# A two-block hybrid layer on one Trainium2 core: mixers that begin with keys and values, one scaling of the keys of both directions, and a planner that keeps two engines off one port

## Chip, core and metric

The kernel runs on one core of a Trainium2 chip. The metric is the device time of one execution in microseconds. Engines are named as in the profile: PE (TensorE matmul), PEld (its weight load), DVE (VectorE), ACT (ScalarE), POOL (GpSimd), SP (the queue that issues the DMAs).

## The reference

Two blocks run one after the other on `x` of 512 tokens by 1024, all in float32. The first mixes dilated attention, a gated linear attention and block attention, then a feed-forward net. The second has two layers (`DEPTH_2 = 2`); beside `x` it carries a context of 256 tokens, which leaves an output only in the first layer. A layer of the second block, cut to its core:

```python
ux = hx @ w_in[l]; uc = hc @ w_in[l]            # columns: fourier, q, k, v, two gates, i, hq, g
fx = fourier_mix(col(ux, OFF_FOURIER, FOURIER_W), w_four[l])
ax, ac = attention_group(ux, uc, ...)           # keys of context and x together
rx, rc = hgrn_group(ux, uc, ...)                # two directions, chunked scan
x = x + g_a * (jnp.concatenate([fx, ax, rx], axis=-1) @ w_out[l])
x = x + g_f * swiglu(rmsnorm_2(x) * (1 + sc_f) + sh_f, w_gate[l], w_up[l], w_down[l])

# one direction of the scan in hgrn_group (the second runs over flipped tokens):
cum = jnp.cumsum(lf, axis=2); last = cum[:, :, -1:, :]
s_new = jnp.exp(last[:, :, 0, :])[..., None] * s + einsum(kc * jnp.exp(last - cum), vc)
att = jnp.einsum('bhtd,bhsd,bhtsd->bhts', qc, kc, decay)   # decay = exp(cum_t - cum_s), causal
o = einsum(qc * jnp.exp(cum), s) + einsum(att, vc)
```

## The kernel before

**Order and planner.** The program is written as many small generators (tasks). `Sched.run` (L564) holds a clock for each engine, and at each step emits the operation that could start first by its own prices. An operation made by `alt(...)` may go to one of two engines, and the planner takes the one that would end sooner; `copy_any` is such a pair of DVE and ACT, and many `tensor_tensor` are pairs of DVE and POOL. What it emits is fixed: each engine executes its list in that order, and waits between engines are semaphores on data alone. So prices and rules of the planner change no arithmetic, but they set the order on each engine and which engine gets an operation. All instructions show line 543, the one line that emits them.

**The flag that the change sets.** An `Op` has a mark `port` (L242): true for a POOL operation with an input, and for a DVE operation with two or more SBUF inputs that are more than one column wide, or a DVE copy or `tensor_scalar` from SBUF to SBUF. `emit` notes in `s.port` when the last such operation of DVE and of POOL ends. With `LOCK` true, `run` (L595) lets a marked operation begin, in the plan, only after the last marked one of the other engine. With `LOCK` false it ignores them.

**The second block's mixers.** `layer` (L2543) spawns the tasks and feeds matrix products to PE through `mix_in` (L2321). That takes the column groups of `w_in` in a fixed order: four gates first, then `ORDER2` (L150): `i` (the scan's values), `kv`, `hq` (the scan's queries), `q0`, `fo`, `q1`, `g`. `prep` (L157) lays the weights out in memory in the same order. The context of layer 0 runs earlier, between pieces of the first block, in its own order `ORDER2C`. `kv_to` (L1919) normalises the keys per head on DVE, ACT and POOL; `stack_k` (L795) then transposes them on PE, splits them in two parts and copies halves across partitions by DMA. Weights come as 512 KB tiles (`raw`), which ACT and DVE split into two parts (`wu`).

**The scan.** `hgrn` (L2094) runs, for two pairs of heads (`hgp`), one task `seg` for each 256 tokens. A segment holds `K` (keys of both directions side by side, 256 columns each), `Q`, and decay products. It climbs seven levels, `lev` = 1, 2, 4, ... 64. At each level it copies the keys that are needed together (`bidir_gram`, L2058), forms 32 thin products on PE (`low_gram`, 16 for each of two heads; `cross_grams` from level 32 on), and scales keys and queries by decay products (`bidir_level`, L2042) for the next level. The segments with an output are 2 for the context in layer 0 and 4 for `x` in each layer; layer 1's context has 2 without an output. All are chains: a level's products need the level before. PE's list puts dense products of other tasks between the thin ones.

Of the kernel before, what the change touches and what calls it, by code (L numbers as in the profile page):

```python
# [13 lines left out]
ALU = mybir.AluOpType  # L14
# [3 lines left out]
P = 128  # L18
T = 512
TC = 256  # L20
# [89 lines left out]
def tilesA(w):  # L110
    k, n = w.shape
    return w.reshape(k // P, P, n // P, P).transpose(2, 1, 0, 3).reshape(n // P, P, (k // P) * P)
# [23 lines left out]
def pairs(units):  # L136
    return np.ascontiguousarray(np.concatenate(units, 0))
# [9 lines left out]

FF1 = (4,) * 8
FF2 = (4, 4, 4, 4, 6)
ORDER2 = ("i", "kv", "hq", "q0", "fo", "q1", "g")  # L150
ORDER2C = ("i", "kv", "hq", "g", "q0", "q1", "fo")
ORDER1 = ("q", "k", "v0", "p0", "v1", "v2", "p1", "p2", "p3", "v3", "p4", "p5", "r0", "r1")
QPERM = np.concatenate([np.concatenate([np.arange(64 * j, 64 * j + 64), np.arange(64 * (j + 4), 64 * (j + 4) + 64)])
# [3 lines left out]
def prep(i):  # L157
# [40 lines left out]
    for l in range(2):  # L198
# [6 lines left out]
        a[f"w2in{l}"] = pairs([tilesA(x)[t:t + 1] for t in range(2) for x in (ff, fb)]  # L205
                              + [parts[n] for n in ORDER2])
        wo = i["w_out_2"][l]
# [90 lines left out]
def _op(eng, fn, args, kw):  # L298
    aps = [x for x in args if is_ap(x)] + [x for k, x in kw.items() if is_ap(x) and k != "accum_out"]
    outs = keys(args[0])  # L300
    if "accum_out" in kw:
        outs += keys(kw["accum_out"])
    if fn == "tensor_tensor_reduce":
        outs += keys(args[-1])
    ins = all_keys(aps[1:])
    n = max(free_size(a) for a in aps)
    table = None
    if eng == "dve":
        per = 1.04
        if fn in ("tensor_copy", "tensor_scalar", "memset") and not any(in_psum(a) for a in aps):  # L310
            per = 0.52
        if fn == "reciprocal":
            per = 6.6
        cost, lat = 62 + n * per + 62 * any(is_ap(a) and free_size(a) == 1 and n > 1 for a in args[2:]), 130
    elif eng == "act":
        extra = sum(1 for k in ("bias", "scale") if is_ap(kw.get(k))) + (fn == "mul" and is_ap(args[2]))
        cost, lat = 90 + n / 1.2 + 90 * extra + (60 if "accum_out" in kw else 0), 160
        for a in args:
            if not is_ap(a) and a in TABLES:
                table = TABLES[a]  # L320
    elif eng == "pool":
        cost, lat = 115 + n * (2.15 if fn == "tensor_tensor" else 3.7), 150
        if fn == "memset":
            cost = 200 + n
    elif eng == "sp":
        b = 4 * free_size(args[0]) * args[0].shape[0]
        cost, lat = max(b / 360.0, 460), 2300
    else:
        raise ValueError(eng)
    op = Op(eng, [(fn, args, kw)], cost, lat, ins, outs, table)  # L330
    if eng == "dve":

        sb = sum(1 for a in aps[1:] if not in_psum(a) and free_size(a) > 1)
        op.port = sb > 1 or (fn in ("tensor_copy", "tensor_scalar") and sb > 0 and not in_psum(args[0]))
    return op


def V(fn, *a, **k):
    return _op("dve", fn, a, k)
# [6 lines left out]
def G(fn, *a, **k):  # L346
    return _op("pool", fn, a, k)
# [6 lines left out]
def alt(*ops):  # L354
    ops[0].alt = ops[1:]
    return ops[0]
# [44 lines left out]
def zigzag(v, off, dims):  # L401

    return bass.AP(tensor=v.tensor, offset=v.offset + off, ap=[list(v.ap[0])] + [list(d) for d in dims if d[1] > 1 or d is dims[-1]])
# [32 lines left out]
class Sched:  # L436
# [127 lines left out]
    def run(s):  # L564
        while s.tasks:
            best = None
            progress = False
            for t in list(s.tasks):
# [22 lines left out]
                if isinstance(p, Op):  # L591
                    first = None
                    for o in (p,) + tuple(p.alt or ()):
                        ready = s.ready_of(o)
                        if LOCK and o.port:  # L595
                            ready = max(ready, s.port["pool" if o.eng == "dve" else "dve"])
# [27 lines left out]
class Kernel:  # L624
# [1417 lines left out]
    def bidir_level(s, K, Q, src, so, nbl, tot, no, lev):  # L2042


        m = nbl // 2
        sv = src[:, so:so + 2 * nbl].rearrange("p (d b two) -> p d b two", d=2, two=2)
        for d in range(2):
            kv = K[:, d * TC:(d + 1) * TC].rearrange("p (b two l) -> p b two l", two=2, l=lev)[:, :, d, :]
            t = sv[:, 1 - d, :, 1 - d][:, :, None].to_broadcast([P, m, lev])
            yield alt(V("tensor_tensor", kv, kv, t, ALU.mult), G("tensor_tensor", kv, kv, t, ALU.mult))  # L2050
        if Q is not None:
            qv = zigzag(Q, 0, [[2 * lev, m], [TC + lev, 2], [1, lev]])
            t = zigzag(src, so + 1, [[2, m], [nbl - 1, 2], [0, lev]])
            yield alt(V("tensor_tensor", qv, qv, t, ALU.mult), G("tensor_tensor", qv, qv, t, ALU.mult))
        nv = tot[:, no:no + 2 * m].rearrange("p (d b) -> p d b", d=2)
        yield V("tensor_tensor", nv, sv[:, :, :, 0], sv[:, :, :, 1], ALU.mult)
# [331 lines left out]
    def ctx_layer0(s, adaf):  # L2388
# [11 lines left out]
        seq = s.wseq("w2in0")  # L2400
        seq = seq[:4] + [seq[4 + 2 * ORDER2.index(n) + i] for n in ORDER2C for i in range(2)]
        uf_ = [Fut() for _ in seq]
# [140 lines left out]
    def layer(s, L, adaf, cs=None):  # L2543
# [12 lines left out]
        s.spawn(s.fourier(l, st.uf, T, "c_dft512", mix[0:2], st.mixh[0:2]), 3, "fourx")  # L2556
        yield from s.mix_in(l, L.sts, s.W, ORDER2)
        s.q.mark(f"layer {l} w_in end")
# [177 lines left out]
THIN = (0.7, 500.0, 1.0)  # L2736
TABLE = 1000.0
MARGIN = {"pe": 60.0, "act": 60.0, "dve": 60.0}
LOCK = False
ROOM = {"dense": 4, "bias": 6, "stackk": 4, "pair": 4}  # L2740


# [14 lines left out]
```

## Time and profile before

| | |
|---|---|
| time of 3 runs | 2283.43, 2284.42 (median), 2286.66 us |
| the profiled execution's own time | 2282.22 us |
| its span, first to last instruction | 2280.1 us |
| granted TensorE clock, mean over the span | 0.993 |
| busy: PE, DVE, ACT, POOL | 2222.6, 1559.9, 918.6, 214.3 us |

The page says what each engine did over the span; the views of the trace say it of one stretch or one line. PE's busy time is modelled and counts some short waits as work, so its idle time is a lower bound of what PE waits. Dense stages (both feed-forward nets) show PE busy all the time; the stretches in which it isn't are those of the scan.

### The profile page before, as it was taken

What the parts mean: (1) busy time and instruction counts of PE and PEld (TensorE: products, weight loads), DVE (VectorE), ACT (ScalarE), POOL (GpSimd) and SP (SyncE); (2) the same over time, 40 slices, a digit from 0 to 9 for tenths busy, and PEclk for the clock granted to TensorE, in tenths of its full rate; (3) what the DMA queues carried; (4) which work ended last, traced back from release to release, by engine and by line L of the source; (5) the groups of instructions that cost most, each with busy time, mean ns of one, the idle gap of its engine ahead of it and who ended that gap; (6) DMA issues with size and microseconds to landing.
All of it is one profiled execution on the core that took longest, in us unless ns stands there. A gap on an engine that the chain in (4) does not pass through costs nothing.

```text
span 2280.1 us, 42611 instructions
## 1 busy us (share of the span) xinstructions
PE 2222.6 (97%) x17065; PEld 1930.2 (85%) x17065; DVE 1559.9 (68%) x3665; ACT 918.6 (40%) x1679; POOL 214.3 (9%) x286
## 2 busy tenths in 40 slices
PE   8999999999999989999999999999989999999998
PEld 6877987888887978799888888889978889888887
DVE  6878877797888678798765433556768776444445
ACT  5455645442224436664212111124536655222223
POOL 0010014110000061110000000000153100000000
PEclk9999999999999989999999999999999999999999
DMA  5455444434444611234433212333221223222223
GB/s 185 145 152 171 167 155 131 144 130 162 147 153 150 199 61 48 93 115 146 148 128 123 102 65 86 126 130 125 105 80 39 75 74 131 93 101 93 99 96 111
DMA packets 92118, 272.72 MB, mean 120 GB/s; under 512 B 10944, under 2 KB 20952, under 8 KB 91920
## 3 DMA queue, kind: packets, MB, share of 16 engines
q1 hardware_dynamic: 91920, 269.99, 35.4%
q8 instruction: 135, 2.21, 0.4%
q14 instruction: 63, 0.52, 0.1%
HBM read 253.66 MB, written 7.38 MB: 114 GB/s over the span
## 4 chain that ended last, share of the span: by engine, by line
PE 87%; DVE 8%; ACT 2%; issue 2%; DMA 1%; POOL 0%; SPq 0%; DVEq 0%; ACTq 0%; POOLq 0%
PE psm L543 67%; PE psx L543 17%; DVE slot L543 6%; PE psd L543 3%; DVE wu L543 2%; ACT slot L543 1%; ACT wu L543 1%; POOL slot L543 0%; DVE sm L543 0%; DMA raw<-w1in 0%; DMA slot<-ctx 0%; DMA slot<-x 0%; DVE at L543 0%; DMA slot<-slot 0%; DMA rawc<-w2in 0%
## 5 line engine op out<-in xcount | busy, mean ns | idle before, releaser
L543 PE MATMUL psm<-slot,wu 128*128 128x256 f32 (+1 forms) x8415 | 1547.3, 342 | 11.7 <-DVE slot L543 9.9
L543 PEld LDWEIGHTS psm<-slot,wu 128*128 128x128 f32 x8415 | 1310.1, 190 | 194.8 <-DVE slot L543 13.6
L543 ACT CAST wu<-raw 128x1024 fp32r<-128x1024 f32 (+1 forms) x325 | 340.5, 1048 | 879.0 <-PE psm L543 499.0
L543 DVE TENSOR_TENSOR wu<-raw,wu 128x1024 fp32r<-128x1024 f32 (+1 forms) x325 | 413.6, 1273 | 198.6 <-ACT wu L543 192.4
L543 DVE CUSTOM_DVE_ANT_0 slot<-rawc,slot 128x256 f32<-128x256 f32 x640 | 273.2, 427 | 97.9 <-DMA rawc<-wada 87.9
L543 POOL TENSOR_TENSOR slot<-slot,slot 128x128 f32<-128x128 f32 (+2 forms) x196 | 133.8, 710 | 875.7 <-DVE slot L543 732.8
L543 DVE TENSOR_TENSOR slot<-slot,slot 128x256 f32<-128x256 f32 (+6 forms) x318 | 179.7, 571 | 12.3 <-ACT slot L543 9.4
L543 PE MATMUL psm<-wu,slot 128*128 128x256 f32 x1344 | 187.2, 289 | 0.3 <-DVE slot L543 0.3
L543 DVE SCALAR_TENSOR_TENSOR slot<-psm,mods,slot 128x256 f32<-128x256 f32 (+1 forms) x189 | 108.1, 572 | 104.5 <-PE psm L543 103.3
L543 DVE TENSOR_TENSOR slot<-slot,psm 128x512 f32<-128x512 f32 (+1 forms) x200 | 117.7, 595 | 81.3 <-PE psm L543 76.5
L543 PEld LDWEIGHTS psm<-wu,slot 128*128 128x128 f32 x1344 | 168.5, 192 | 4.6 <-issue 2.1
L543 PE MATMUL psx<-slot,wu 128*128 128x512 f32 (+1 forms) x849 | 160.9, 344 | 0.4 <-DVE wu L543 0.4
L543 PE MATMUL psd<-slot,slot 64*32 64x32 f32 (+6 forms) x3584 | 128.3, 220 | 23.4 <-DVE slot L543 10.1
L543 PEld LDWEIGHTS psx<-slot,wu 128*128 128x128 f32 x849 | 134.1, 190 | 18.3 <-DVE wu L543 0.8
L543 PEld LDWEIGHTS psd<-slot,slot 64*32 64x32 f32 (+4 forms) x3584 | 95.9, 119 | 55.6 <-POOL slot L543 23.2
L543 PE MATMUL psx<-slot,slot 128*64 128x128 f32 (+6 forms) x1554 | 122.3, 284 | 2.1 <-DVE slot L543 2.1
L543 PEld LDWEIGHTS psx<-slot,slot 128*64 128x64 f32 (+4 forms) x1554 | 92.3, 142 | 26.6 <-issue 11.9
L543 ACT CAST slot<-slot 128x512 fp32r<-128x512 f32 (+3 forms) x142 | 79.5, 561 | 73.8 <-DVE slot L543 53.4
L543 ACT COPY slot<-psx 128x256 f32<-128x256 f32 (+4 forms) x192 | 78.9, 419 | 74.9 <-PE psx L543 65.9
L543 ACT ACTIVATE slot<-slot 128x256 f32<-128x256 f32 (+1 forms) x150 | 64.9, 456 | 35.0 <-DVE slot L543 31.2
L543 DVE SCALAR_TENSOR_TENSOR slot<-slot,mods,slot 128x256 fp32r<-128x256 f32 (+2 forms) x152 | 72.5, 516 | 4.6 <-ACT slot L543 4.5
L543 ACT ACTIVATE pr<-psd,sm 128x768 f32<-128x768 f32 (+1 forms) x80 | 65.3, 818 | 17.8 <-DVE sm L543 17.2
(100 smaller groups left out, 1365.0 us busy)
## 6 DMA issues: line engine op xcount, KB each, us to landing
rawc<-wada SPq DMA_DIRECT2D x96, 512.0 KB, 4.5
raw<-w2gu SPq DMA_DIRECT2D x88, 512.0 KB, 3.3
raw<-w1ff SPq DMA_DIRECT2D x64, 512.0 KB, 3.3
raw<-w2da SPq DMA_DIRECT2D x56, 512.0 KB, 3.3
raw<-w2in SPq DMA_DIRECT2D x36, 512.0 KB, 3.7
raw<-w2out SPq DMA_DIRECT2D x24, 512.0 KB, 3.3
raw<-w1in SPq DMA_DIRECT2D x23, 512.0 KB, 3.6
rawc<-w2in SPq DMA_DIRECT2D x18, 512.0 KB, 3.4
```

Of the source, the lines that this page charges most:

```text
L543: r = getattr(eng, fn)(*a, **k)
```

## The change

Three things. `ORDER2` begins with `kv`, then `i`; the weights in memory are permuted with it. In `bidir_level` the two multiplications that scale the keys of one direction each (128 columns) become one over both (256 columns). `LOCK` becomes true.

```diff
-ORDER2 = ("i", "kv", "hq", "q0", "fo", "q1", "g")
+ORDER2 = ("kv", "i", "hq", "q0", "fo", "q1", "g")
...
         sv = src[:, so:so + 2 * nbl].rearrange("p (d b two) -> p d b two", d=2, two=2)
-        for d in range(2):
-            kv = K[:, d * TC:(d + 1) * TC].rearrange("p (b two l) -> p b two l", two=2, l=lev)[:, :, d, :]
-            t = sv[:, 1 - d, :, 1 - d][:, :, None].to_broadcast([P, m, lev])
-            yield alt(V("tensor_tensor", kv, kv, t, ALU.mult), G("tensor_tensor", kv, kv, t, ALU.mult))
+        kv = zigzag(K, 0, [[2 * lev, m], [TC + lev, 2], [1, lev]])
+        t = zigzag(src, so + nbl + 1, [[2, m], [-nbl - 1, 2], [0, lev]])
+        yield alt(V("tensor_tensor", kv, kv, t, ALU.mult), G("tensor_tensor", kv, kv, t, ALU.mult))
...
-LOCK = False
+LOCK = True
```

The last line is used here, in `run`, which is unchanged:

```python
                        if LOCK and o.port:
                            ready = max(ready, s.port["pool" if o.eng == "dve" else "dve"])
```

Over the whole program PE's instructions are the same ones in another order; POOL has 282 instructions of the kernel's own before and 128 now, DVE 2977 and 3060, ACT 1519 and 1506. For the stretches of the scan, between the same two numbers of matmuls on PE: in the first half of layer 1's `x` scan POOL goes from 46 to 17 and DVE from 70 to 64; in its second half POOL from 24 to 11, DVE from 88 to 104. Layer 0's `x` scan is alike (POOL 44 to 17 and 26 to 11, DVE 66 to 63 and 91 to 103). Around the context's scan POOL goes from 43 to 19 and DVE from 122 to 140. From there to layer 0's scan POOL goes from 24 to 6 and DVE from 552 to 573.

How it looks on POOL at the start of layer 1's `x` scan (slot_3087 and slot_3088 are the `K` of two segments, slot_3174 and slot_3177 their `Q`, slot_3085, 3086, 3175 and 3178 decay products). Before:

```order
L543 TENSOR_TENSOR slot_3087_17083<-slot_3087_17083,slot_3085_17081 128x128 x2
L543 TENSOR_TENSOR slot_3174_17779<-slot_3174_17779,slot_3085_17081 128x128x2
L543 TENSOR_TENSOR slot_3088_17084<-slot_3088_17084,slot_3086_17082 128x128 x2
L543 TENSOR_TENSOR slot_3087_17083<-slot_3087_17083,slot_3175_17781 128x64x2 x2
L543 TENSOR_TENSOR slot_3174_17779<-slot_3174_17779,slot_3175_17781 128x64x2x2
L543 TENSOR_TENSOR slot_3088_17084<-slot_3088_17084,slot_3178_17787 128x64x2 x2
```

Now:

```order
L543 TENSOR_TENSOR slot_3087_17034<-slot_3087_17034,slot_3085_17032 128x128x2
L543 TENSOR_TENSOR slot_3088_17035<-slot_3088_17035,slot_3086_17033 128x128x2
L543 TENSOR_TENSOR slot_3087_17034<-slot_3087_17034,slot_3175_17724 128x64x2x2
L543 TENSOR_TENSOR slot_3088_17035<-slot_3088_17035,slot_3178_17733 128x64x2x2
L543 TENSOR_TENSOR slot_3177_17731<-slot_3177_17731,slot_3178_17733 128x64x2x2
```

Each pair of key scalings (a row with x2) is one row over both directions; one scaling of a `Q` stands among the rows in either.

On PE near the end of the same scan (rows with 32x32 x16 or 64x64 x8 are the thin products of one level; 128x256 into psm are dense fill). Before:

```order
L543 MATMUL psd_3254_18598<-slot_3202_17992,slot_3098_17158 32x32 x16
L543 MATMUL psm_3244_18519<-wu_3188_17893,slot_3042_16790 128x256 x2
L543 MATMUL psm_3244_18519<-wu_3188_17893,slot_3043_16791 128x256
L543 MATMUL psd_3255_18607<-slot_3213_18170,slot_3099_17159 32x32 x16
L543 MATMUL psm_3245_18520<-wu_3188_17893,slot_3027_16730 128x256 x2
L543 MATMUL psm_3245_18520<-wu_3188_17893,slot_3028_16731 128x256
L543 MATMUL psm_3245_18520<-wu_3188_17893,slot_3031_16751 128x256 x2
L543 MATMUL psm_3245_18520<-wu_3188_17893,slot_3032_16752 128x256
L543 MATMUL psd_3257_18659<-slot_3202_17992,slot_3098_17158 64x64 x8
L543 MATMUL psd_3258_18679<-slot_3213_18170,slot_3099_17159 64x64 x8
```

Now (the psd rows 128x512 and 128x256 are attention scores, the psx rows 128x256 the Fourier mixer):

```order
L543 MATMUL psd_3295_18698<-slot_3142_17464,slot_3260_18587 128x512
L543 MATMUL psd_3295_18698<-slot_3143_17465,slot_3260_18587 128x512
L543 MATMUL psd_3295_18698<-slot_3124_17313,slot_3260_18587 128x256 x2
L543 MATMUL psx_3311_18758<-slot_3049_16780,slot_3256_18564 128x256
L543 MATMUL psx_3311_18758<-slot_3050_16782,slot_3273_18663 128x256
L543 MATMUL psx_3311_18758<-slot_3049_16780,slot_3256_18564 128x256
L543 MATMUL psx_3311_18758<-slot_3050_16782,slot_3273_18663 128x256
L543 MATMUL psm_3271_18661<-wu_3235_18308,slot_3042_16748 128x256 x2
L543 MATMUL psm_3271_18661<-wu_3235_18308,slot_3043_16749 128x256
L543 MATMUL psd_3313_18767<-slot_3208_17999,slot_3099_17110 32x32 x16
```

The last levels of the last segment now have attention, Fourier and dense products ahead of them, where before a few dense products stood between the last levels of two segments.

## Rows read from the trace of the kernel before

**Rows 1.** The page: busy time of each engine; the chain that ended last.

```profile
PE 2222.6 (97%) x17065; PEld 1930.2 (85%) x17065; DVE 1559.9 (68%) x3665; ACT 918.6 (40%) x1679; POOL 214.3 (9%) x286
PE 87%; DVE 8%; ACT 2%; issue 2%; DMA 1%; POOL 0%; SPq 0%; DVEq 0%; ACTq 0%; POOLq 0%
```

**Rows 2.** Busy time by stretch: context scan, dense, layer 0's scan, before layer 1's scan, it.

```profile
core 0: us, PE busy (x) PEld busy (x) DVE busy (x) ACT busy (x) POOL busy (x), PEclk, DMA share, GB/s
360.00:400.00 40.00, 35.71 (x630) 25.11 (x630) 36.76 (x109) 20.89 (x44) 26.63 (x38) 1.00 0.40 125
434.00:521.00 87.00, 87.00 (x487) 71.11 (x486) 77.67 (x239) 36.93 (x96) 11.05 (x13) 1.00 0.41 140
800.00:847.00 47.00, 40.02 (x845) 31.54 (x843) 35.62 (x77) 18.22 (x40) 33.49 (x48) 0.92 0.21 70
847.00:891.00 44.00, 41.95 (x607) 37.59 (x608) 39.08 (x98) 28.39 (x70) 15.29 (x24) 0.93 0.16 50
1636.00:1680.00 44.00, 43.13 (x357) 41.42 (x356) 17.93 (x44) 14.54 (x29) 4.10 (x6) 1.00 0.19 66
1680.00:1714.00 34.00, 27.06 (x786) 20.48 (x786) 30.05 (x67) 13.37 (x31) 30.09 (x44) 0.98 0.21 65
1714.00:1757.00 43.00, 41.30 (x600) 36.92 (x597) 38.02 (x92) 27.84 (x70) 14.95 (x24) 0.93 0.16 51
```

**Rows 3.** Waits in 1680 to 1757: engine line <- releaser: us, times, longest.

```profile
PE psd L543 <- DVE slot L543: 4.8, 6, 1.3
...
PEld psd L543 <- POOL slot L543: 8.8, 11, 1.7
...
ACT slot L543 <- POOL slot L543: 13.0, 8, 3.5
```

**Rows 4.** POOL by form in 1680 to 1757: busy us, mean ns of one | idle before.

```profile
L543 POOL TENSOR_TENSOR slot<-slot,slot 128x128 f32<-128x128 f32 x46 | 24.2, 548 | 5.0 <-DVE slot L543 2.7 <-PE psd L543 1.5 <-POOL slot L543 0.8
L543 POOL TENSOR_TENSOR slot<-slot,slot 128x256 f32<-128x256 f32 x12 | 9.8, 822 | 0.5 <-PE psd L543 0.4
```

**Rows 5.** DVE by form in 1680 to 1740.

```profile
L543 DVE TENSOR_TENSOR slot<-slot,slot 128x256 f32<-128x256 f32 x16 | 10.2, 635 | 0.1
L543 DVE TENSOR_TENSOR wu<-raw,wu 128x1024 fp32r<-128x1024 f32 x5 | 7.0, 1391 | 0.0
...
L543 DVE TENSOR_TENSOR slot<-slot,slot 128x128 f32<-128x128 f32 x10 | 4.0, 420 | 0.0
L543 DVE TENSOR_TENSOR slot<-slot 128x64 f32<-128x64 f32 x4 | 2.8, 700 | 0.0
```

**Rows 6.** DVE by form in 1880 to 2280, where POOL does nothing.

```profile
L543 DVE TENSOR_TENSOR wu<-raw,wu 128x1024 fp32r<-128x1024 f32 x78 | 95.5, 1224 | 99.4 <-ACT wu L543 99.3
...
L543 DVE TENSOR_TENSOR slot<-slot,slot 128x256 f32<-128x256 f32 x10 | 4.2, 420 | 0.3
```

**Rows 7.** Instructions in order of time, 1704 to 1714: start us, us, engine.

```profile
1707.46 4.60 POOL L543 TENSOR_TENSOR slot<-slot,slot 128x128 f32<-128x128 f32 x7 [0.58 <-POOL slot L543]
1712.29 0.88 POOL L543 TENSOR_TENSOR slot<-slot,slot 128x128 f32<-128x128 f32 x2 [0.23 <-DVE slot L543]
```

**Rows 8.** The same time on DVE.

```profile
1708.90 1.18 DVE L543 TENSOR_TENSOR slot<-slot,slot 128x128 f32<-128x128 f32 x1
...
1713.52 0.28 DVE L543 TENSOR_TENSOR slot<-slot,slot 128x128 f32<-128x128 f32 x1
```

**Rows 9.** Stretches at a lowered clock, columns as in rows 2.

```profile
842.00:854.00 12.00, 11.18 (x237) 8.60 (x235) 11.56 (x32) 6.45 (x20) 8.94 (x16) 0.57 0.01 5
1712.00:1721.00 9.00, 7.90 (x209) 6.50 (x209) 8.28 (x25) 3.10 (x10) 5.93 (x13) 0.62 0.02 4
```

**Rows 10.** Order of time before layer 1's scan: transposes of `stack_k`, first thin products.

```profile
1679.01 0.44 PE L543 MATMUL psx<-c_ident,slot 128*128 128x128 f32 x2 [0.87 <-DVE slot L543]
...
1681.45 0.35 PE L543 MATMUL psd<-slot,slot 64*32 64x32 f32 x32
```

## Prediction

> **What bounds the kernel now.** I read the page first, then a table of busy time by stretch, then the waits, forms and single instructions of the stretch that stood out. The page says that PE is busy 97% of the span and carries 87% of the chain that ended last; POOL is busy 9% and has no share of that chain [rows 1]. The change leaves PE's instructions as they are, so what can be won is PE's waiting and the time that it spends at a lowered clock. The table by stretch shows where that is [rows 2]. In the dense stretch PE is busy 87.00 of 87 us, whatever DVE and POOL do. In the scans it is not: it idles 4.3 us in the context's, 7.0 and 2.1 us in the two halves of layer 0's, 6.9 and 1.7 us in those of layer 1's, 22.0 us in all. [...]
>
> Who makes PE wait there: in layer 1's scan its weight loads wait 8.8 us for POOL, its matmuls 4.8 us for DVE, and ACT, which copies keys for the next level, 13.0 us for POOL [rows 3]. In the first half POOL is busy 30.09 of 34 us and DVE 30.05, PE only 27.06: two helpers are as good as full, and POOL is the slow one. In the second half DVE is the fullest helper, 38.02 of 43 [rows 2].
>
> Part of that load is the two helpers in each other's way. A DVE multiplication of 128 columns with both inputs in SBUF takes 1.18 us when it starts inside seven POOL instructions, and 0.28 us a few us later, when POOL is idle [rows 7, 8]. Over 60 us of that scan 16 of 256 columns average 635 ns, 10 of 128 columns 420 ns, 4 of 64 columns 700 ns and 5 weight splits 1391 ns [rows 5]; where POOL does nothing, 256 columns take 420 ns and a split 1224 [rows 6]. With 0.28 us for the 128 columns, and at most that for the 64, this is 16 x 0.215 + 10 x 0.14 + 4 x 0.42 + 5 x 0.167 = 7.4 us of DVE time lost in 60.
>
> **The change part by part.** The sum is made against the profiled execution: 2282.22 us, of which 2280.1 are its span. The median of the runs, 2284.42, lies 2.2 above it, and I add that at the end.
>
> *Keys scaled together.* There are 12 segments with 7 levels: 168 instructions of 128 columns become 84 of 256. On POOL a pair costs 2 x 548 ns, one of 256 columns 822 [rows 4]; on DVE one costs 420 to 635 ns [rows 5, 6]. A level of the chain gets 0.27 us (POOL both times) to 0.68 us (POOL before, DVE now) shorter. None of this stands on PE's path by itself; it counts where PE waits for the level. The worst case, a pair that ran on DVE and POOL side by side (548 ns) and is now one on POOL (822), loses 0.27 us for a level.
>
> *Exclusive reads in the plan.* POOL keeps 17 of 46 instructions in the first half of layer 1's scan, at 822 ns some 14 us in place of 30.09; DVE goes from 70 to 64 there, so both helpers get lighter. What comes last then is PE itself, 27.06 us, so at most 6.9 us go. I take 4: the chain's latency stays, and the first levels keep as little fill between them as before. Layer 0's first half has the same order, 7.0 us of idle and 3.8 us of clock: I take 5.5, since a PE that waits less may also keep its clock. In the second halves DVE gets 12 and 16 instructions more, at 420 ns 5.0 and 6.7 us, and loses the collisions (26 of those 60 us hold 3.2 us of them); its free time is 4.9 and 5.0 us [rows 2]. So nearly nothing is left to win by load; the longer fill ahead of the last levels and the clock are worth 1 us in each. Bounds of each: the idle and clock of its row on one side, 1 to 2 us lost on the other. The context's scan has 4.3 us of idle; POOL goes from 43 to 19 there, DVE from 122 to 140, over twice as much dense work: 2 us.
>
> *Moved in the dense stretches.* 18 accumulations and the like leave POOL for DVE between the context's scan and layer 0's. They are of up to 512 columns; their cover is PE at 87.00 of 87 us, with DVE at 77.67 [rows 2]. I cost them at nothing. Without that cover, 18 at about the 0.64 us that my row has for 256 columns under collision would be 11 us of DVE time spread over 400.
>
> *Keys and values first.* The same weight tiles come through SP in the same number, since memory is permuted with the order; `kv` and `i` both precede `hq`, which the scan waits for. So the start of the scan does not move. What moves is the keys' normalising, the transposes and the four DMAs of `stack_k`: they now run under the products of `i`, in a stretch where DVE is busy 17.93 of 44 us [rows 2]. Before, two of the transposes let PE wait 0.87 us, 2.4 us ahead of the first thin products [rows 10]. I take 0.5 us. The copies of `i` move the other way, but are needed only at a segment's end. Nothing queued behind SP's DMAs is new to that stretch. Bounds: 0.9 won, and 1 lost if the copies of `i` now meet the scan's first levels.
>
> The sum: 5.5 + 4 + 1 + 1 + 2 + 0.5 = 14.0 us. Span 2266.1, own time 2268.2, and with the 2.2 us to the median **2270.4 us**.
>
> **The rivals.** *More goes than I take.* If the waits of the scans were all due to POOL and the collisions, idle (22.0 + 0.9) and clock (10.5) would both go: 33 us, 2251 us. For it: POOL and DVE are both full where PE waits most. Against: 3.8 us of the idle are in second halves, where POOL is not full. Chance 0.10, for all times under 2260.
>
> *The plan isn't what runs.* The exclusion exists only in the plan; no semaphore holds DVE back when POOL reads. If real durations drift, the two still meet, and what PE waits for is the chain's latency, not load. Then only 0.27 us a level on a few levels is won, and moved work gives it back elsewhere: 2280 to 2289, likeliest 2284. For it: 28 POOL instructions are left in layer 1's scan, and DVE is busier in the second half. Against: they are far fewer. [...] Chance 0.20.
>
> *DVE becomes the bound.* One mechanism, in the second halves and the context's scan: DVE gets 12, 16 and 18 instructions more. At 420 ns these are 5.0, 6.7 and 7.6 us against 4.9, 5.0 and 3.2 us of free time [rows 2]. If the collisions stay, 0.1 + 1.7 + 4.4 = 6.2 us stick out on the path, and with about 2 us of copies and evictions that queue behind them on DVE the kernel takes 8 us more: 2292 us. It decides from the point at which DVE has no idle time in these stretches. For it: the keys' copies and PE's psum buffers both wait on DVE there. Against: 7.4 us of collisions per 60 us should mostly go. [...] Chance 0.16.
>
> **How the numbers follow.** Forecast (2260 to 2279) 0.54, more 0.10, no change 0.20, slower 0.16. About 0.2% (4.6 us) can be told from no change. Range: 2252 to 2292, from the end of the first rival to that of the last. Faster 0.64, same 0.20, slower 0.16.
>
> **What would show it.** Right: in layer 1's scan PE's weight loads wait under 4 us for POOL (8.8 now), DVE's 256-column multiplications average under 500 ns, the first half takes about 30 us in place of 34, and the clock falls less often around the scans. Wrong: PE idles as long as before but for DVE; DVE is busy over 95% of a second half; the lowered clock comes at new places; or PE loses its full occupation in a dense stretch.

## The result, and the profile after

The changed kernel takes 2251.45 us (median of 4 runs, 2246.94 to 2253.5), the kernel before 2285.54 beside it: a ratio of 0.9844, interval 0.9817 to 0.987. It is faster by 34 us where 14 were forecast, and half a microsecond below the range. The profiled execution took 2253.5 us, with a span of 2251.7; it is the slowest of the four, so its span shows 28.4 us of the gain.

The page of the kernel after, busy times and chain (as in [rows 1]):

```profile
PE 2215.3 (98%) x17065; PEld 1927.7 (86%) x17065; DVE 1556.4 (69%) x3748; ACT 913.4 (41%) x1666; POOL 129.2 (6%) x132
PE 90%; DVE 5%; DMA 2%; ACT 1%; issue 1%; SPq 0%; DVEq 0%; ACTq 0%
```

POOL has lost 85 us of work, DVE has 83 instructions more and is no busier, and PE is busy 7.3 us less.

Busy time by stretch after the change, columns as in [rows 2]: the two halves of layer 0's scan, its attention and what follows, the same of layer 1:

```profile
805.00:836.00 31.00, 29.02 (x748) 23.00 (x748) 28.80 (x68) 12.92 (x32) 16.76 (x16) 0.96 0.21 69
836.00:878.00 42.00, 40.76 (x651) 36.41 (x650) 39.78 (x106) 25.31 (x63) 10.69 (x11) 0.99 0.17 52
878.00:966.00 88.00, 86.56 (x771) 73.93 (x771) 69.79 (x146) 63.02 (x136) 9.06 (x7) 1.00 0.23 79
1663.00:1693.00 30.00, 27.91 (x788) 21.95 (x788) 29.05 (x65) 12.99 (x32) 17.14 (x16) 1.00 0.17 57
1693.00:1734.00 41.00, 39.54 (x611) 35.28 (x608) 39.42 (x107) 25.86 (x64) 9.86 (x10) 1.00 0.17 53
1734.00:1823.00 89.00, 88.08 (x787) 75.49 (x785) 67.83 (x139) 59.87 (x124) 7.60 (x6) 1.00 0.20 66
```

Of the kernel before, layer 0's whole scan, and the attention stretches, which stand in no row ahead of the prediction:

```profile
812.00:891.00 79.00, 71.11 (x1384) 59.48 (x1383) 68.32 (x160) 41.76 (x100) 45.07 (x68) 0.91 0.18 56
891.00:983.00 92.00, 89.20 (x781) 75.36 (x780) 69.00 (x136) 61.02 (x133) 7.59 (x6) 1.00 0.22 71
1757.00:1852.00 95.00, 92.24 (x817) 78.12 (x817) 70.54 (x137) 61.28 (x132) 7.60 (x6) 1.00 0.18 57
```

The scans fall from 79 to 73 us and from 77 to 71. The attention falls from 92 to 88 and from 95 to 89, though POOL does at least as much there as before (9.06 and 7.60 us; 7.59 and 7.60), at the full granted clock (1.00) both times. These windows don't hold quite the same products (817 and 787 in layer 1); at equal work, in the table below, the attention falls by 4.7 and 4.8 us up to the end of the output projection. That second fall is in no term of the forecast.

The waits of layer 1's scan, 1663 to 1734, as in [rows 3]:

```profile
ACT slot L543 <- POOL slot L543: 8.4, 4, 3.5
...
PEld psd L543 <- issue: 4.5, 11, 0.9
...
PE psd L543 <- DVE slot L543: 2.0, 5, 0.8
```

PE's weight loads, which waited 8.8 us for POOL, have no such row left, and its matmuls wait 2.0 us for DVE in place of 4.8. DVE's and POOL's multiplications in the same stretch, as in [rows 4, 5]:

```profile
L543 DVE TENSOR_TENSOR slot<-slot,slot 128x256 f32<-128x256 f32 x30 | 15.5, 536 | 0.0
...
L543 DVE TENSOR_TENSOR slot<-slot,slot 128x512 f32<-128x512 f32 x6 | 6.6, 1112 | 0.0
...
L543 POOL TENSOR_TENSOR slot<-slot,slot 128x256 f32<-128x256 f32 x26 | 27.0, 1055 | 57.7 <-DVE slot L543 25.8 <-issue 22.1 <-PE psd L543 7.9
```

The two still collide. DVE takes 536 ns for 256 columns and 1112 for 512, where the same lists without POOL's work take 449 and 685 (g3_after_dve, below). Of POOL's 26, 24 overlap a TENSOR_TENSOR of DVE in time and take 1090 ns on average; the other two take 636. The plan keeps them apart on paper only, and yet the kernel is faster.

**One table for all runs.** PE executes the same products in every kernel here, so its row (the list of its instructions) can be cut at points of equal work, and the traces tell when each point is reached. C is the stretch around the context's scan (195.9 us before), S0 and S1 the scans of `x` in the two layers (78.9 and 77.7), A0 and A1 what follows each up to the end of the output projection, attention above all (147.6 and 145.3). The columns give how much longer each takes than in the kernel before, in us, in the profiled executions. "Run" is the longest piece of PE's row in the attention, layer 0 / layer 1, without a dense product (one by a weight tile `wu`); it is an estimate, with 0.23, 0.12 and 0.11 us for products of 512, 256 and 128 columns: from one start to the next, in rows of one form, their medians in the traces before and after are 227, 120 and 109 ns, and a dense stretch has 90 of the first in 20 us. It counts next to nothing for products whose weights are 64 columns wide, of which 24 of 128 columns take 1.53 us in the traces, so it serves to compare kernels and not as a duration. The rows are in the order in which the kernels ran; the experiments are told below.

| kernel | us | C | S0 | A0 | S1 | A1 | run |
|---|---|---|---|---|---|---|---|
| before | 2285.5 | 0 | 0 | 0 | 0 | 0 | 6.1 / 6.1 |
| after | 2251.5 | -5.6 | -6.3 | -4.7 | -6.8 | -4.8 | 4.8 / 4.8 |
| e1_lock | 2260.8 | -3.2 | -10.6 | +3.7 | -6.7 | -4.8 | 10.0 / 4.8 |
| e2_merge | 2313.1 | +2.2 | +0.2 | +13.3 | +1.7 | +13.1 | 15.4 / 15.4 |
| e3_order | 2283.0 | -0.2 | -1.4 | 0.0 | +0.6 | 0.0 | 6.1 / 6.1 |
| e4_nolock | 2308.6 | +0.7 | -0.7 | +11.8 | +1.1 | +12.9 | 15.4 / 15.4 |
| e5_nomerge | 2263.1 | -3.3 | -11.1 | +5.3 | -8.3 | -2.6 | 10.0 / 5.6 |
| e6_noorder | 2262.9 | -4.9 | -8.6 | +2.3 | -5.0 | -5.7 | 7.2 / 3.8 |
| e7_price | 2309.3 | -0.2 | -0.3 | +6.5 | +0.9 | +7.3 | 9.2 / 9.2 |
| e8_nopool | 2296.8 | -4.8 | -9.9 | +20.7 | -13.1 | +17.1 | 19.1 / 25.3 |
| f1_merge_fourier_first | 2307.0 | +2.0 | +2.9 | +13.3 | +5.2 | +2.4 | 10.7 / 10.8 |
| f2_after_fourier_first | 2256.8 | -5.5 | -4.3 | -3.5 | -4.0 | -6.1 | 6.0 / 4.5 |
| f3_after_fourier_last | 2287.5 | -5.3 | -9.5 | +19.2 | -5.8 | +12.4 | 18.9 / 11.9 |
| g1_before_dve | 2294.3 | +2.5 | +0.5 | +1.6 | +3.1 | +0.4 | 6.1 / 6.1 |
| g2_merge_dve | 2315.1 | +1.0 | -0.8 | +14.3 | +1.5 | +14.5 | 15.4 / 15.4 |
| g3_after_dve | 2258.6 | -4.6 | -7.1 | -1.6 | -5.9 | -3.6 | 4.8 / 4.8 |
| h1_after_thin | 2254.6 | -5.0 | -5.4 | -4.5 | -5.2 | -2.9 | 4.4 / 4.4 |
| h2_before_thin | 2276.3 | -1.0 | -1.8 | -0.4 | -1.0 | 0.0 | 6.1 / 6.1 |
| g4_after_pool | 2269.2 | -4.6 | 0.0 | -4.7 | -0.7 | -4.8 | 4.8 / 4.8 |
| h3_after_act | 2242.2 | -5.5 | -9.2 | -4.3 | -7.5 | -4.9 | 3.9 / 3.9 |

The 641 us of dense work from A0 to S1 agree within 1.1 us in all kernels but three (e6 +2.2, e7 +2.8, g4 +4.7). Of the 28.4 us of the profiled executions, S0 and S1 are 13.1, A0 and A1 9.5, C 5.6 and the stretch between C and S0 2.9; the rest of the program gives 2.7 back.

Each entry is from one execution. Cut at equal numbers of products in place of equal work, most entries move by under 2 us, all by at most 2.5 except in e8 (5). Where the lists of all engines are the same, the stretches agree well: the changed kernel, f2 and f3 lie within 0.3 us in C. Ahead of C they don't: f3 and g4, with the same lists up to there, reach C 9 us apart, so a difference ahead of C in one execution says nothing, the 2.7 us among them.

One thing runs through the table. In every kernel planned with `LOCK` true S0 and S1 are at least 4 us shorter than before, g4 alone excepted; in none planned with it false is either shorter by over 1.8.

### The profile page after: what moved, and what is told of

Same layout as the page of the kernel before. It is cut to its first block, busy times and chain, and to the rows that moved or that the text cites. A ratio compares the mean times of both kernels' runs of the same rounds, so it can differ in the third digit from the quotient of the medians.

```text
span 2251.7 us, 42381 instructions
## 1 busy us (share of the span) xinstructions
PE 2215.3 (98%) x17065; PEld 1927.7 (86%) x17065; DVE 1556.4 (69%) x3748; ACT 913.4 (41%) x1666; POOL 129.2 (6%) x132
## 4 chain that ended last, share of the span: by engine, by line
PE 90%; DVE 5%; DMA 2%; ACT 1%; issue 1%; SPq 0%; DVEq 0%; ACTq 0%
PE psm L543 70%; PE psx L543 17%; PE psd L543 4%; DVE slot L543 3%; DVE wu L543 1%; ACT wu L543 1%; ACT slot L543 0%; DMA raw<-w1in 0%; DVE at L543 0%; DVE sm L543 0%; DMA rawc<-wada 0%; DMA slot<-ctx 0%; DMA slot<-slot 0%; DMA slot<-x 0%; DMA rawc<-w2in 0%
## 5 line engine op out<-in xcount | busy, mean ns | idle before, releaser
L543 PEld LDWEIGHTS psm<-slot,wu 128*128 128x128 f32 x8382 | 1305.5, 190 | 192.3 <-DVE slot L543 11.9
L543 DVE TENSOR_TENSOR wu<-raw,wu 128x1024 fp32r<-128x1024 f32 (+1 forms) x325 | 399.9, 1231 | 187.5 <-ACT wu L543 183.2
L543 DVE TENSOR_TENSOR slot<-slot,slot 128x256 f32<-128x256 f32 (+4 forms) x347 | 196.8, 574 | 21.0 <-ACT slot L543 18.3
L543 PE MATMUL psm<-wu,slot 128*128 128x256 f32 x1392 | 193.3, 289 | 0.5 <-DVE wu L543 0.5
L543 PEld LDWEIGHTS psm<-wu,slot 128*128 128x128 f32 x1392 | 174.7, 192 | 5.0 <-issue 1.9
L543 PE MATMUL psx<-slot,wu 128*128 128x512 f32 (+1 forms) x882 | 167.2, 345 | 0.1
L543 PEld LDWEIGHTS psx<-slot,wu 128*128 128x128 f32 x882 | 140.0, 190 | 19.1 <-DVE wu L543 0.3
L543 POOL TENSOR_TENSOR slot<-slot,slot 128x256 f32<-128x256 f32 (+1 forms) x82 | 83.7, 1033 | 973.7 <-DVE slot L543 787.7
L543 PE MATMUL psx<-slot,slot 128*64 128x128 f32 (+5 forms) x1554 | 122.7, 285 | 1.5 <-DVE slot L543 1.4
L543 PEld LDWEIGHTS psx<-slot,slot 128*64 128x64 f32 (+3 forms) x1554 | 91.2, 140 | 23.4 <-issue 10.8
L543 ACT COPY slot<-psx 128x512 f32<-128x512 f32 (+5 forms) x194 | 80.1, 426 | 73.1 <-PE psx L543 65.7
```

The costliest lines, as they stand in the source:

```text
L543: r = getattr(eng, fn)(*a, **k)
```

## The experiments

### One part alone, one part undone

Three kernels have one part of the change each.

```diff
e1_lock:   -LOCK = False
           +LOCK = True
e2_merge:  the lines of bidir_level in the diff above, alone
e3_order:  -ORDER2 = ("i", "kv", "hq", "q0", "fo", "q1", "g")
           +ORDER2 = ("kv", "i", "hq", "q0", "fo", "q1", "g")
```

> The kernel before with the exclusive plan alone (LOCK true); order and the two key scalings as before. Theory 1 (POOL's slow, colliding work made PE wait; the plan takes it away): most of the 34 us gained, 2257 to 2266 us. Theory 2 (the merged scaling shortens the chain of each level, and that is what counts): 2275 to 2288. Theory 3 (the plan of one fixed list is luck; any of the three edits shifts times by some 10 us without regard to POOL): anything, and the gains of the three edits do not follow POOL's load.

> The kernel before with one scaling for the keys of both directions alone. Theory 1: POOL stays as busy in the scans, so little changes, 2278 to 2288 us. Theory 2: the chains are shorter, 2255 to 2270. Theory 3: anything.

> The kernel before with keys and values ahead of i alone. Theory 1 and 2: 2280 to 2288 us, since nothing of the scan's load moves. Theory 3: anything. If the new order is what gave the attention stretches behind the scans their 5 us each, then 2270 to 2277 and these stretches are shorter here.

Exclusive planning alone: 2260.82 us, ratio 0.9897 (0.9876 to 0.9918), 23 us of the 34. The merged scaling alone: 2313.07 us, 1.0129 (1.0108 to 1.015), slower by 30 us. Keys and values first alone: 2282.98 us, 0.9996 (0.9983 to 1.0009). Then the change with one part taken back:

```diff
e4_nolock:   -LOCK = True
             +LOCK = False
e5_nomerge:  the two multiplications of bidir_level as before
e6_noorder:  ORDER2 as before
```

> The changed kernel with the exclusive plan undone (LOCK false). Theory 1: most of the gain is lost, 2272 to 2288 us. Theory 2: most of it stays, 2252 to 2265. Theory 3: anything.

> The changed kernel with the key scalings of the two directions apart again. Theory 1 (POOL's slow, colliding work; the exclusive plan takes it away): 2251 to 2262 us, since the plan still keeps POOL light. Theory 2 (shorter chains by the merged scaling): 2268 to 2285. Theory 3 (luck of one list): anything.

> The changed kernel with i ahead of keys and values again. Theory 1 and 2: 2250 to 2258 us, the order is worth a few us at most. If the order is what shortened the attention stretches behind the scans: 2260 to 2266, and those stretches are as long as before.

Without exclusive planning 2308.61 us (1.0106, 1.0086 to 1.0126), without the merged scaling 2263.1 (0.991, 0.989 to 0.993), without the order 2262.94 (0.9908, 0.9888 to 0.9928). Of these six, e2 and e4 came out slower than any range that was named for them. So the parts don't add. The merged scaling costs 30 us by itself and gains 12 beside the other two; the order gains nothing by itself and 11 beside the other two. What a part does to its own instructions isn't what it is worth; the table says where most of the difference sits, in A0 and A1, behind the scans that the merged scaling touches.

### Another price for GpSimd, and no GpSimd

```diff
e7_price (after, LOCK = False):
-        cost, lat = 115 + n * (2.15 if fn == "tensor_tensor" else 3.7), 150
+        cost, lat = 270 + n * (2.15 if fn == "tensor_tensor" else 3.7), 150
e8_nopool (after):
-    ops[0].alt = ops[1:]
+    ops[0].alt = tuple(o for o in ops[1:] if o.eng != "pool")
```

> The changed kernel with LOCK false, but with 155 ns more for each POOL instruction in the planner's price, about what they took beyond it in the kernel before. It separates two parts of theory 1: if it is enough that the plan knows how slow POOL is (fewer instructions there, more fill on PE), 2252 to 2264 us; if the plan has to keep the two apart in time, 2268 to 2282.

> The changed kernel with no choice of POOL at all: every such operation goes to DVE, and POOL has only its first memsets. Theory 1 in the form that POOL is a nuisance: 2245 to 2256 us. If DVE is the bound in the scans, so that what stays on POOL is needed: 2260 to 2285 us, with DVE busy over 95% of the scans' second halves.

A truer price for POOL (545 and 820 ns for 128 and 256 columns, which took 548 and 822 in [rows 4]) gave 2309.31 us (1.0115, 1.0094 to 1.0136); a plan without POOL 2296.82 (1.0057, 1.0035 to 1.0079); both are slower than any range that was named. With the truer price the scans aren't shorter at all, though POOL has less of them than before (42 instructions in each layer's scan for 68). In the plan without POOL the scans are among the shortest, 23 us less in both layers together, and the attention is 38 us longer. There, what was won in the scan is lost behind it.

### Where the dense products lie in the attention

Sorted by "run", the table's A0 and A1 are nearly sorted too. The reading that the next kernels test: the output projection needs the Fourier mixer's outputs first, so a Fourier transform that PE finishes late leaves it no dense product to put between the softmax steps. Three kernels change only that task's priority in `layer`.

```diff
-        s.spawn(s.fourier(l, st.uf, T, "c_dft512", mix[0:2], st.mixh[0:2]), 3, "fourx")
+        ... 1, "fourx")      f1_merge_fourier_first (on e2_merge), f2_after_fourier_first (on after)
+        ... 5, "fourx")      f3_after_fourier_last (on after)
```

> The kernel before plus the one scaling of keys for both directions (2313.07 us when alone), and in both layers the Fourier transform of the second block asks with priority 1 in place of 3. The scans keep the order they have in that run; the transform's last product on TensorE moves ahead, and the longest run of matmul work in the attention stretch of TensorE's list without a dense product in it falls from 15.4 us to 10.7 (layer 0) and 10.8 (layer 1). Theory A (the attention stretch is as long as this run makes it, because the output projection's first products need the transform, and until then nothing dense can be put between the softmax steps): the two stretches fall from 107 and 108 us to 96 to 102 each, and the time to 2290 to 2302 us. Theory B (GpSimd and VectorE colliding decide, and the Fourier transform's place is of no matter): 2309 to 2317, the stretches as they were.

> The changed kernel (2251.45 us) with priority 1 in place of 3 for the Fourier transform. Its longest run without a dense product goes from 4.8 and 4.8 us to 6.0 and 4.5. Theory A (the run sets the attention stretch): layer 0's stretch 0 to 4 us longer, layer 1's within 2, the time 2250 to 2257. Theory B (no matter): 2248 to 2254. The run tells little between the two; it is there as the other half of the run with the merged scaling: what gains some 16 us there must gain nothing here.

> The changed kernel (2251.45 us) with priority 5 in place of 3 for the Fourier transform, so that it comes after everything but the loads of tables; GpSimd, exclusive planning and the merged scaling as in the changed kernel. The longest run of attention work on TensorE without a dense product grows from 4.8 us to 18.9 in layer 0 and to 11.9 in layer 1. Theory A (the run sets the attention stretch): layer 0's second-block stretch 15 to 22 us longer than in the changed kernel, layer 1's 7 to 13 longer, the time 2273 to 2286, and the gain of the change nearly gone with every scan as fast as in the changed kernel. Theory B (the gain of the change is one of GpSimd's collisions and waits alone): 2248 to 2256.

They took 2306.96 us (1.0094, 1.0078 to 1.0109), 2256.81 (0.9874, 0.9858 to 0.9891) and 2287.48 (1.0017, 1.0008 to 1.0026). The third shows it best: with scans as fast as in the changed kernel, A0 and A1 are 24 and 17 us longer (15 to 22 and 7 to 13 expected) and the whole gain is gone. Its attention stretch in layer 0, columns as in [rows 2], then PE's waits there:

```profile
869.00:983.00 114.00, 98.33 (x813) 77.47 (x810) 73.27 (x151) 67.74 (x151) 6.89 (x6) 0.99 0.16 52
```

```profile
PE psx L543 <- DVE slot L543: 6.6, 7, 1.6
PE psx L543 <- ACT slot L543: 5.6, 10, 1.4
PE psd L543 <- ACT pr L543: 2.9, 3, 1.4
```

PE idles 15.7 of 114 us, most of it for softmax steps of ACT and DVE, where the changed kernel idles 1.4 of 88. The first run bears the theory out by half: A1 falls from 13.1 to 2.4 us, but A0 stays at 13.3, the scans get 2.7 and 3.5 us longer, and the total falls by 6 us where at least 11 were expected. What holds layer 0 there wasn't found.

### The engine moved, the order kept

Up to here each kernel that changed POOL's work changed PE's order with it. In these, the plan stays and only the engine of an instruction is exchanged when it is emitted. The rows of PE, ACT and SP are, word for word, those of the kernel that they start from.

```diff
g1_before_dve (on before), g2_merge_dve (on e2_merge), g3_after_dve (on after):
-            r = getattr(eng, fn)(*a, **k)
+            r = getattr(s.eng["dve"] if e == "pool" and fn == "tensor_tensor" else eng, fn)(*a, **k)
g4_after_pool (on after):
-        eng = s.eng[e]
+        eng = s.eng["pool" if e == "dve" and who[:2] == "hg" and any(o.eng == "pool" for o in op.alt or ()) else e]
```

> The kernel before with its own plan, but each multiplication that the plan gave to GpSimd runs on VectorE, at the place in VectorE's row that its planned start gives it. TensorE's, ScalarE's and SyncE's rows are those of the kernel before, word for word. Theory P (GpSimd itself, slow and in VectorE's way, costs the time that the exclusive plan gains): most of the 24 us of exclusive planning alone comes without a new plan: 2256 to 2268 us, the scans of both layers 6 to 10 us shorter each and the attention stretches 0 to 5 shorter. Theory L (the new plan's order on TensorE brings the gain): no more than the waits for GpSimd in the scans goes, 2274 to 2290 us, and the clock is lowered in the same places as before.

> The kernel with the merged scaling alone (2313.07 us; attention stretches 13 us longer in each layer than in the kernel before), with its own plan and GpSimd's multiplications run on VectorE; TensorE's, ScalarE's and SyncE's rows stay as they are. Theory P: the loss of 28 us goes, 2260 to 2285 us. Theory L: the attention stretches stay 10 to 15 us too long in each layer, since TensorE's row has only 17 us of dense products there where it has 26 in the kernels before and after, and the time is 2300 to 2316 us.

> The changed kernel (2251.45 us) with its own plan and GpSimd's remaining 126 multiplications run on VectorE; all other rows as they are. Theory P: still 3 to 10 us to gain, 2241 to 2248 us. Theory L: 2247 to 2257 us, the collisions that are left lie beside full TensorE. That VectorE has become the bound there would show as more than 2258 us.

Taking POOL's multiplications away gains nothing in any of the three: 2294.33 us (1.0038, 1.0027 to 1.0049), 2315.07 (1.0125, 1.0106 to 1.0144), 2258.6 (0.9888, 0.986 to 0.9917). The first is 9 us slower than the kernel before, past both ranges that were named; the third is just past the 2258 us that were set down as the sign that DVE has become the bound. Of layer 1's scan in the first: its first half, columns as in [rows 2]; two forms of DVE in 1689 to 1749; the waits in 1689 to 1769.

```profile
1689.00:1724.00 35.00, 29.50 (x789) 22.74 (x787) 31.56 (x106) 12.56 (x29) 0.00 (x0) 0.85 0.20 63
```

```profile
L543 DVE TENSOR_TENSOR slot<-slot,slot 128x128 f32<-128x128 f32 x56 | 13.7, 282 | 0.1
L543 DVE TENSOR_TENSOR slot<-slot,slot 128x256 f32<-128x256 f32 x28 | 12.5, 445 | 0.0
```

```profile
ACT slot L543 <- DVE slot L543: 21.5, 13, 4.9
PEld psd L543 <- issue: 7.2, 13, 1.6
PEld psd L543 <- ACT slot L543: 6.9, 9, 2.1
...
PE psd L543 <- DVE slot L543: 4.7, 5, 2.0
PE psd L543 <- ACT slot L543: 2.9, 4, 1.2
```

The collisions are gone (282 and 445 ns against 420 and 635 in [rows 5]), and so is every wait for POOL; but ACT, which waited 13.0 us for POOL and 3.9 for DVE, waits 21.5 for DVE, and PE's weight loads wait 6.9 us for ACT where they waited 8.8 for POOL. What POOL did now queues on DVE, which is busy 31.56 of 35 us: PE's row asks for its products at the same points, and their inputs come as late. In layer 1 the granted clock is lower besides (0.85 of 35 us is 5.2 lost, 0.98 of 34 was 0.7 in [rows 2]); layer 0's scan, with the mean clock of before (0.91), takes 79.4 us for 78.9. The second run shows that the loss of the merged scaling is one of the order: A0 and A1 stay 14 us too long. In the third the scans keep their gain (-7.1 and -5.9) with no POOL at all; DVE's multiplications in 1660 to 1740:

```profile
L543 DVE TENSOR_TENSOR slot<-slot,slot 128x256 f32<-128x256 f32 x56 | 23.4, 449 | 0.0
...
L543 DVE TENSOR_TENSOR slot<-slot,slot 128x512 f32<-128x512 f32 x6 | 4.0, 685 | 0.0
```

The fourth puts POOL's load back into the changed kernel's order.

> The changed kernel (2251.45 us) with its own plan, but every multiplication of the scans that may run on either engine runs on GpSimd: 174 of the scans' multiplications there in place of 72 (188 in the kernel before). TensorE's, ScalarE's and SyncE's rows are those of the changed kernel, word for word. Theory P (GpSimd's slowness and collisions cost what the exclusive plan gains): the scans of layers 0 and 1 go back to 79 and 77 us as before, the context's too, 2262 to 2275 us, and TensorE's weight loads wait for GpSimd again, some 9 us in layer 1's scan. Theory L (TensorE's order brings the gain, whoever multiplies): 2249 to 2258 us.

It took 2269.16 us (0.993, 0.9903 to 0.9956), as the theory on GpSimd had it. Layer 1's scan and attention, columns as in [rows 2], and the weight loads' waits in 1680 to 1757:

```profile
1678.00:1710.00 32.00, 26.97 (x734) 20.86 (x733) 21.28 (x41) 11.24 (x26) 31.04 (x34) 0.95 0.16 53
1710.00:1755.00 45.00, 41.89 (x658) 37.05 (x659) 42.57 (x94) 27.39 (x70) 23.06 (x29) 1.00 0.16 49
1755.00:1845.00 90.00, 89.08 (x799) 76.30 (x799) 68.11 (x140) 60.39 (x126) 10.17 (x8) 1.00 0.21 66
```

```profile
PEld psd L543 <- POOL slot L543: 10.0, 13, 1.7
```

POOL is busy 31.04 of 32 us, the weight loads wait 10.0 us for it, and S0 and S1 lose nearly all that the change had gained there (0.0 and -0.7; -1.6 and -1.7 when cut at equal numbers of products), while C, A0 and A1 keep theirs to within 1 us (-4.6, -4.7, -4.8). So the gain falls into two. The scans' 13.1 us need the new order and a POOL that isn't loaded as before: POOL emptied in the old order brings nothing (g1), and the new order with POOL's load put back brings next to nothing there (g4). What a light POOL would bring in the old order with DVE no fuller than before wasn't run; in g1 DVE carries the difference. The 9.5 us of the attention and most of the 5.6 around the context's scan are the order's alone, that of PE, ACT and SP held together.

### More room among the scan's products, and a version faster than both

```diff
h1_after_thin (on after), h2_before_thin (on before):
-THIN = (0.7, 500.0, 1.0)
+THIN = (0.5, 500.0, 1.0)
h3_after_act (on after):
-        cost, lat = 90 + n / 1.2 + 90 * extra + (60 if "accum_out" in kw else 0), 160
+        cost, lat = 90 + n / 1.2 + 90 * extra + (60 if "accum_out" in kw else 0), 220
```

> The changed kernel (2251.45 us) with one number of the planner changed: a dense product pays back 0.5 of its cost, not 0.7, of what thin products (under 40 ns each in the planner's price) have run up. TensorE's row then has 44.4 us of other work among the scan's products in layer 0 (40.0 in the changed kernel, 27.6 before) and 85.4 in layer 1 (81.0; 68.2), and the longest run of attention work without a dense product is 4.4 us in both layers (4.8). GpSimd has 8 instructions more. Theory L (TensorE's order decides: other work among the scan's products, dense products among the attention's): 0 to 6 us faster than the changed kernel, 2245 to 2252. Theory P (GpSimd's share decides): 2251 to 2256.

> The kernel before with the same number changed, 0.7 to 0.5; no exclusive plan, no merged scaling, the old order of the mixers. TensorE's row from the attention on is that of the kernel before, with the same longest run (6.1 us); in the scans 34.6 us of other work lie among the products of layer 0 (27.6 before) and 75.2 in layer 1 (68.2). GpSimd has 309 instructions, 27 more than before. Theory L: the scan stretches are 5 to 10 us shorter in each layer and the attention stretches as before, 2264 to 2276 us, though GpSimd and its collisions grow. Theory P: 2283 to 2292.

> The changed kernel (2251.45 us) with one number of the planner changed: it counts 220 ns, not 160, from the end of a ScalarE instruction to its result. TensorE's row then has at most 3.9 us of attention work in a row without a dense product in both layers (4.8 in the changed kernel, 6.1 before). If that run sets the attention stretch, the stretches from the scan's end are 0 to 3 us shorter than in the changed kernel, and the time is 2244 to 2254 us with the scans as in the other exclusive plans. If it doesn't, the stretches lie anywhere within 5 us of the changed kernel's and the time between 2250 and 2264.

More work among the scan's products gave 2254.55 us in the changed kernel (0.988, 0.9865 to 0.9894), no gain where the theory on the order expected up to 6 us, and 2276.31 in the kernel before (0.9969, 0.9957 to 0.998). The second gains 8 us, but S0 and S1 give 2.8 where 10 to 20 were expected; the weight loads still wait for POOL in layer 1's scan, 1676 to 1748:

```profile
PEld psd L543 <- POOL slot L543: 7.5, 9, 2.3
```

How far apart the products stand is thus a small part of what makes the new order better; which trait of it brings the scans' share stays open. The third kernel took 2242.19 us (2240.06 to 2242.55; 0.9815, 0.9793 to 0.9836), the fastest of all: its runs lie below all of the changed kernel's, though the two weren't run side by side. Its scans, 797 to 867 and 1653 to 1723:

```profile
797.00:867.00 70.00, 67.82 (x1380) 57.77 (x1378) 65.58 (x168) 38.12 (x94) 28.20 (x27) 1.00 0.19 63
1653.00:1723.00 70.00, 67.65 (x1384) 57.82 (x1384) 65.31 (x166) 38.92 (x96) 27.55 (x27) 0.98 0.17 55
```

They take 70 us each where the changed kernel takes 73 and 71; A0 and A1 are as there, so the shorter run, 3.9 us, won nothing more. Up to the beginning of C its profiled execution is 6.6 us ahead of the changed kernel's; that may be chance, since f3, with the changed kernel's own lists up to there, is 5.2 us ahead of it too.

## Why the prediction was right and wrong

**The scans: the sizes about right.** First halves: 4.8 and 4.1 us gained (5.5 and 4 forecast), second halves 1.5 and 2.7 (1 and 1), 13.1 in place of 11.5. Cut at equal numbers of products, the halves give 4.3, 4.0, 3.6 and 3.8. The signs came as listed: layer 1's first half takes 30.4 us, the weight loads' wait for POOL is under 4 us, and the granted clock falls less: 0.91 of 79 us is 7.1 us lost in layer 0 before; 0.96 of 31 and 0.99 of 42 are 1.7 after. The clock's 3.8 us in the term for layer 0's first half, and 10.5 us for the four halves, are worked out from [rows 2]: 0.08 of 47 us, 0.07 of 44, 0.02 of 34 and 0.07 of 43. That a PE that waits less keeps its clock was the author's guess, and no run shows it by itself: over layer 0's scan PE idles 7.9 of 79 us at a clock of 0.91 before, 3.2 of 73 at 0.98 after and 2.2 of 70 at 1.00 in h3, but also 7.9 of 79 at 0.96 in g4.

**The reason behind them only half right.** The forecast let the gain come from POOL's load and from collisions. g1 took both away, with the load moved to DVE, and gained nothing; g4 put the load back into the new order and lost the scans' gain. So in these runs a lighter POOL gained only together with the new order, to which the forecast gave no share. The 256-column multiplications average 536 ns, not under 500, and against g3's 449 collisions stay at (536 - 449) x 30 = 2.6 us in those alone. The sign of the third rival came too: DVE is busy 39.42 of 41 us in a second half, 96%. It did not become the bound: PE's products wait 2.0 us for DVE in the whole scan, 4.8 before.

**The step that failed: the terms stopped at the scans' end.** The table of stretches [rows 2] had the scans and a dense stretch, and "moved in the dense stretches" was costed at nothing. That is right for the 641 us from A0 to S1, which agree within 1 us. But between a scan and the dense stage lies the attention, 92 and 95 us in the two layers, with PE idle 2.8 us in each, and this was neither looked at nor costed. The lists shown with the change even had attention, Fourier and dense products shifted ahead of the scan's last levels. What the attention gained measured 9.5 us, more than the idle itself, so part of it was in time that the page counts as busy. In e8, e2 and f3 it is up to 38 us the other way: the largest unknown of the case, with no bound in the range. That the order sets it is shown by g2, g3 and g4; that the trait of the order is the place of the dense products is shown by f3 and only half by f1.

**The context: mis-sized.** 2 us were put on its scan's 4.3 us of idle; C gives 5.6, of which 4.6 stay with POOL's load put back. The 2.9 us between C and S0 were in no term; the instructions moved there were costed at nothing.

**Keys scaled together.** Costed at a shorter chain, and at 0.27 us a level at worst. Alone it costs 30 us, through the order behind the scans (e2, g2); beside the other two parts it gains 12. The price of the instruction decides neither. **Keys and values first:** 0.5 forecast, nothing measured alone.

**The rivals.** The first gave the time measured, 2251, by luck: it added the idle and the clock of the scans, 33 us, while the scans of `x` made 13.1, C 5.6, and the rest came from places that it left out. "The plan isn't what runs" is right on the collisions, and wrong that no gain is left then. In layer 1's scan of the changed kernel 15 of DVE's 30 multiplications of 256 columns overlap one of POOL's and average 645 ns, the other 15 428, so one that meets POOL loses 0.22 us on average, where POOL's take 1055 ns; and by g1 the collisions alone aren't what decides. With PE's order held, g1 and g3 agree on work moved from POOL to DVE: no gain in either (2294.33 us where the kernel before took 2285.1 beside it; 2258.6 where the changed kernel took 2251.45).

## What to carry to other kernels

Where a planner fixes every engine's order, a change of its rules or of one instruction is worth what the whole new order is worth, and here that was anything from 30 us lost to 23 won for one part alone, much of it behind the place that was touched; cost every stretch whose order moves, above all those in which the bound engine needs filler between steps of a chain. To tell an engine's load from the order, keep the order and exchange only the engine: here that split one gain into a part that needs both and a part that is order alone. Of two helpers that were both nearly full (30.09 and 30.05 of 34 us), emptying the slow one into the other gained nothing in the old order (g1, 9 us slower). And one order is one draw: a planner's constant changed by 60 ns gave another 9 us, for no reason that was found.

## What the runs showed that was not expected

Both sides of a collision lose. POOL's multiplication of 256 columns takes 1090 ns where it overlaps a TENSOR_TENSOR of DVE and 636 in the two that don't; DVE's of 512 columns take 1112 ns beside POOL and 685 in the same lists without POOL's work. And a stretch with PE idle 1.4 of 88 us and one with 15.7 of 114 come from kernels that differ in one priority of one task.
